# Sixteen high products, then sixteen low ones: the order inside a block of weights

## The chip, the core and the metric

The kernel runs on one core of one Trainium2 chip. The metric is the device time of one execution in microseconds (us). A core has a matrix engine (TensorE, PE in the profile, with its weight loads listed apart as PEld), three engines for elementwise work (VectorE or DVE, ScalarE or ACT, GpSimd or POOL), and queues that issue transfers (SP for SyncE).

## The reference

Two layers of a decoder act on 256 tokens of 1024 features, in float32. A layer is

```
h = rmsnorm(x); proj = h @ w_in            # 1024 -> 8192 columns: conv b, c, u; q, k; v, g; ga, gb
y_conv = short_conv(b, c, u) @ w_conv_out
y_ret  = (silu(g) * norm(retention(q, k, v))) @ w_ret_out
x = x + (sigmoid(ga) * y_conv + sigmoid(gb) * y_ret) @ w_o
x = x + square(relu(rmsnorm(x) @ w_up)) @ w_down   # 1024 -> 4096 -> 1024
```

and a last rmsnorm follows. Nearly all the work is the products with the weights: some 40 million multiplications per token and part, each weight used once against all 256 tokens.

## The kernel before

Activations are kept with features on the 128 partitions and tokens along the free axis. For accuracy every operand of a large product is held as two parts, a high one (the value cast to the fp32r type, ACT, line 99) and a low one (what the cast left over, DVE, line 100). A product then takes three terms: high by high, high by low, and low by high. `Parts.at(k)` gives the 128 features of tile k as `[high 256 tokens | low 256 tokens]`, 512 columns side by side.

The weights come from memory in 152 blocks of 1 MB, each 1024 rows by 256 columns, as 16 weight tiles of 128 x 128. `load_block` issues the transfer and splits the block in two halves: for each half one ACT cast makes the high part and one DVE subtraction makes the low part. `next_block` does this two blocks ahead (AHEAD = 2); there are three raw buffers and three buffers for the parts.

`proj` takes one block (or four, in the last product of a layer) against an activation. For weight tile (k, j) it issues two matmuls: the high weights against all 512 columns, into the whole PSUM bank j, and the low weights against the 256 high columns, into the second half of bank j. A matmul is always preceded by the load of its weights, so a block is 32 loads and 32 matmuls. PE therefore sees 512, 256, 512, 256 and so on. 140 of the 152 blocks pass through `proj`. The others are eight blocks of v through `proj_tokens` (four at the head of each layer), where the roles of weights and activation are exchanged, and four at the end through `proj_one`, where all matmuls have 256 columns. `collect` (ACT copy, DVE add) brings a result out of PSUM; `ps_main` has three buffers of two banks.

Between blocks `run_waiting` puts small products: scores and values of the retention, sums of squares (`column_sums`, lines 219 and 220, two 512-column matmuls one after the other, or two of 256).

The order of the instructions on each engine is not the text's alone: a planner replays the program with its own costs when it is built, and takes, among what it thinks ready, what comes first in the text. Where it thought an activation late, the matmuls stand in another order than the text's (the first block behind a norm, for one); elsewhere the text's order holds.

Of the kernel before, what the change touches and what calls it, by code (L numbers as in the profile page):

```python
# [18 lines left out]
P = 128  # L19
# [12 lines left out]

# Columns of w_in in the order in which they are used, 256 at a time.
Q0, K0, V0, G0, GA0, GB0 = 3072, 3584, 4096, 5120, 6144, 7168
# [8 lines left out]
BLOCKS_PER_LAYER = 32 + 4 * 3 + 16 + 16  # L43
# Layout of the per-feature parameters of a layer.
G_MIX, G_MLP, G_RET, W_CONV, PER_LAYER = 0, 8, 16, 24, 48
# [3 lines left out]
def trunk_kernel(ctx, tc, px, pos, w, cst, mask, out):  # L49
# [31 lines left out]
    class Parts:  # L81
        """1024 features of an activation as two parts whose sum is exact, side by side."""

# [18 lines left out]
    def block_tiles():  # L102
        """A block as it comes, [P, 16, 128], and as two parts whose sum is exact."""
        raw = raw_p.tile([P, 2 * KT, P], F32, tag="raw", name="raw")
        parts = parts_p.tile([P, 2, 2 * KT, P], F32R, tag="parts", name="parts")
        return raw, parts
# [22 lines left out]

    # Small products wait here until the products that hide their inputs' latency are under way.  # L130
    waiting = []
# [15 lines left out]
    def proj(act, n_blocks=1):  # L147
        """256 features of act @ w, features on the partitions: [P, 2, 2, T].

        The products of the high parts are at [:, :, 0], those with a low part at [:, :, 1].  # L150
        """
        ps = ps_main.tile([P, 2, 2, T], F32, tag="mm", name="ps")
        for b in range(n_blocks):
            blk = next_block()
            for k in range(KT):
                a = act[b].at(k)
                for j in range(2):
                    first, end = b == 0 and k == 0, b == n_blocks - 1 and k == KT - 1
                    mm(ps[:, j], blk[:, 0, 2 * k + j, :], a, first, False)
                    mm(ps[:, j, 1], blk[:, 1, 2 * k + j, :], a[:, 0], False, end)  # L160
            run_waiting()
        return ps

    def proj_one(act, plus, n_blocks=2):
        """128 features of act @ w, from blocks of 2048 rows, and the two parts of plus: [P, T]."""
        ps = ps_main.tile([P, T], F32, tag="mm", name="ps1")
        n = 2 * KT
        for b in range(n_blocks):
            blk = next_block()
            for k in range(n):  # L170
                a = act[(b * n + k) // KT].at(k % KT)
                mm(ps, blk[:, 0, k, :], a[:, 0], b == 0 and k == 0, False)
                mm(ps, blk[:, 0, k, :], a[:, 1], False, False)
                mm(ps, blk[:, 1, k, :], a[:, 0], False, b == n_blocks - 1 and k == n - 1)
            if b == 0:
                for part in range(2):
                    mm(ps, ident, plus[:, part], False, False)
            run_waiting()
        return ps

    def proj_tokens(act):
        """256 features of act @ w, tokens on the partitions: [P, 2 (tokens), 2, 256]."""
        ps = ps_main.tile([P, 2, 2, T], F32, tag="mm", name="ps")
        blk = next_block()
        for k in range(KT):
            a = act.at(k)
            for j in range(2):
                c = slice(j * P, (j + 1) * P)
                mm(ps[:, j], a[:, 0, c], blk[:, :, 2 * k:2 * k + 2, :], k == 0, False)
                mm(ps[:, j, 1], a[:, 1, c], blk[:, 0, 2 * k:2 * k + 2, :], False, k == KT - 1)  # L190
        run_waiting()
        return ps

    def collect(ps, t=None):
        """The sum of the two halves of a product."""
        t = t2("sum", "sum", 4) if t is None else t
        nc.scalar.copy(t, ps[:, :, 1, :])  # L197
        nc.vector.tensor_tensor(out=t, in0=ps[:, :, 0, :], in1=t, op=ALU.add)  # L198
        return t

    def newton(y, a, m):
        """y nearer to m ** -0.5"""
        nc.vector.tensor_tensor(out=a, in0=y, in1=y, op=ALU.mult)
        nc.vector.scalar_tensor_tensor(out=a, in0=a, scalar=-0.5, in1=m, op0=ALU.mult, op1=ALU.mult)
        nc.vector.scalar_tensor_tensor(out=y, in0=a, scalar=1.5, in1=y, op0=ALU.add, op1=ALU.mult)

    def rsqrt(y, v, scale, alloc):
        """y = (v * scale + EPS) ** -0.5: a start from the bits, and three Newton steps."""
        m, a = alloc("rs_m"), alloc("rs_a")
        nc.vector.tensor_scalar(out=m, in0=v, scalar1=scale, scalar2=EPS, op0=ALU.mult, op1=ALU.add)  # L210
        nc.vector.tensor_scalar(
            out=y.bitcast(I32), in0=m.bitcast(I32), scalar1=-0.5, scalar2=float(0x5F3759DF), op0=ALU.mult, op1=ALU.add
        )
        for _ in range(3):
            newton(y, a, m)

    def column_sums(o, hi, lo):
        """The sums over the partitions of hi + lo, on every partition of o."""
        nc.tensor.matmul(o, lhsT=ones, rhs=hi, start=True, stop=False)
        nc.tensor.matmul(o, lhsT=ones, rhs=lo, start=False, stop=True)  # L220

    class Norm:
        """RMSNorm whose per-token factor is applied behind the products."""

# [35 lines left out]
        def total(self):  # L260
            """The sum of the squares of each token, on every partition."""
            st = ps_misc.tile([P, T], F32, tag="misc", name=f"{self.name}_st")
# [9 lines left out]

# [1 line left out]
    nc.vector.memset(idle, 0.0)  # L274
    nc.vector.memset(eps, EPS)
    # Any function of the table that the first activations need.
    nc.scalar.activation(eps2, eps, AF.Square)
# [18 lines left out]
    ready.update((i, b[1]) for i, b in enumerate(begun))  # L296
    # The tensor engine's clock rises only under load.
    warm = ps_misc.tile([P, 2 * T], F32, tag="misc", name="warm")
# [10 lines left out]
    def rotation_tables():  # L309
# [21 lines left out]
        nc.gpsimd.tensor_tensor(out=sin_t, in0=u, in1=n_, op=ALU.mult)  # L331
        # The minus sign of the first half of the rows, and the two of the double angle.
        scale(sin_t, sin_t, cst_sb[:, 1:2])
# [3 lines left out]
    for layer in range(DEPTH):  # L337
# [5 lines left out]
        def factors(norm=norm):  # L343
            """Per token: the norm's factor and its square, and the rotation with one or both."""
            rsqrt(rr, norm.total(), 1.0 / D, lambda n: t2(n, "rs", 2)[:, 0, :])
# [6 lines left out]
        if layer == 0:  # L352
# [7 lines left out]
            later(5, nc.sync.dma_start, mask_sb, mask)  # L360
        # The first four blocks do not need them.
        later(4 if layer == 0 else 2, factors)

        qk = stile("qk")
        # What is used against 256 tokens is kept in two parts: [P, 2 (parts), head, ...].
        q_parts, v0_parts = (s8.tile([P, 2, HEADS, T], F32R, tag="s8", name=n) for n in ("q_parts", "v0_parts"))
# [97 lines left out]
        def head_sums(i):  # L464
            """Two heads: the mean of the squares of each token, and its root by table."""
            st = ps_misc.tile([P, 2, T], F32, tag="misc", name="var_ps")
# [7 lines left out]
        def head_out(i):  # L474
            """Two heads: their norm, its gain, and the gate."""
            rs = rm[:, 0, 2 * i:2 * i + 2, :]
# [118 lines left out]

# [1 line left out]
    gf = par_sb[:, DEPTH * PER_LAYER:DEPTH * PER_LAYER + KT]  # L597
# [21 lines left out]
    later(2, sums_of, norm.sum[:, 0, :], True, False)  # L619
    # Brings in the table of the square root ahead of its use.  # L620
    nc.scalar.activation(eps2, norm.sum[:, 0, 0:1], AF.Sqrt)
    for k in (KT - 2, KT - 1):
# [8 lines left out]
        else:  # L631
            sums_of(sq, False, True)
    # A square root by table is the start, one Newton step makes it exact to float32.
    m, r, a = (small.tile([P, 2], F32, tag=n, name=n) for n in ("fin_m", "fin_r", "fin_a"))
# [3 lines left out]
    for c in (slice(0, 1), slice(1, 2)):  # L638
        nc.vector.scalar_tensor_tensor(
            out=a[:, c], in0=r[:, c], scalar=m[:, c], in1=r[:, c], op0=ALU.mult, op1=ALU.mult  # L640
        )
    # -2 times the result; the matrix that spreads it is -1/2 times the identity.
    nc.vector.scalar_tensor_tensor(out=r, in0=a, scalar=3.0, in1=r, op0=ALU.subtract, op1=ALU.mult)
# [14 lines left out]

# [1 line left out]
def _feature_tiles(a):  # L660
    """[..., 1024] -> [128, ..., 8]: feature 128 k + p at [p, ..., k]."""
    a = a.reshape(a.shape[:-1] + (KT, P))
# [3 lines left out]
def _blocks(w, starts, width=256):  # L666
    """Blocks of [8 x 128 rows, 256 columns], each as [128, 8 * 256]."""
    out = []
# [61 lines left out]
```

## Time and profile before

| | |
|---|---|
| median of 3 runs | 896.24 us (895.91 to 896.86) |
| the profiled execution | its span of 896.8 us, first to last instruction, is all the time that the profile gives for it |
| PE busy | 880.4 us, 98% |
| DVE, ACT, POOL busy | 704.1, 503.0, 272.2 us |
| matmuls | 5092 |
| mean granted TensorE clock | 0.988 of full speed |

Matmuls overlap, so the busy time of PE only says that it hardly waits. What one costs is read from the distance between the starts of neighbours, or from a long piece of the chain that ended last: its microseconds by its count of matmuls.

### The profile page before, as it was taken

Reading aid. Unit: us, or ns where it says so; the run is one execution under the profiler, and the core shown is the slowest. Engines: PE = TensorE matmul, PEld = TensorE weight load, DVE = VectorE, ACT = ScalarE, POOL = GpSimd, SP = SyncE. Lnnn points to the kernel's source line nnn. Section 1 sums busy time; section 2 is a strip of 40 time slices with the busy share of each in tenths; the row PEclk is TensorE's granted clock in tenths of the full one; section 3 lists DMA queues with packets and bytes.
Section 4 is the critical chain, followed back from the end, with each engine's and each line's share of the span. In section 5 each row is a group of like instructions: output and inputs, shape, how many; then the busy total and the mean of one; then the engine's idle time right before and its main releaser. Section 6 shows DMA issues by size and latency. Waiting matters only on the chain.

```text
span 896.8 us, 12679 instructions
## 1 busy us (share of the span) xinstructions
PE 880.4 (98%) x5092; PEld 769.0 (86%) x5092; DVE 704.1 (79%) x790; ACT 503.0 (56%) x704; POOL 272.2 (30%) x174
## 2 busy tenths in 40 slices
PE   6999999999999999999999999999999999999996
PEld 4887888888888888888888888888888888888896
DVE  6999999997767976555579999999967888664451
ACT  4645565565455877544444466656644687764440
POOL 4895443261003332100026643415300323220010
PEclk7999999999999999999999999999999999999998
DMA  8544653546444655555545465445655546555521
GB/s 274 192 176 149 227 188 141 178 170 220 185 146 183 235 194 187 200 190 194 190 161 188 141 212 199 153 141 189 235 188 188 188 155 221 190 191 190 191 84 48
DMA packets 24250, 163.00 MB, mean 182 GB/s; under 512 B 2816, under 2 KB 3200, under 8 KB 4992
## 3 DMA queue, kind: packets, MB, share of 16 engines
q1 hardware_dynamic: 23904, 161.68, 50.8%
q8 instruction: 40, 0.66, 0.3%
q10 hardware_dynamic: 288, 0.52, 0.2%
q14 instruction: 18, 0.15, 0.0%
HBM read 161.14 MB, written 1.05 MB: 181 GB/s over the span
## 4 chain that ended last, share of the span: by engine, by line
PE 91%; DVE 3%; POOL 3%; DMA 1%; ACT 1%; issue 1%; SPq 1%; DVEq 0%; POOLq 0%; ACTq 0%
PE ps L145 88%; DVE parts L100 1%; PE o_ps L145 1%; DMA raw<-w 1%; POOL ang L326 1%; PE sc_ps L145 1%; POOL sum L394 1%; DVE rot L380 0%; POOL red L314 0%; DVE rot L379 0%; POOL ang L314 0%; ACT parts L99 0%; POOL v L394 0%; DVE mix L235 0%; POOL qk L381 0%
## 5 line engine op out<-in xcount | busy, mean ns | idle before, releaser
L100 DVE TENSOR_TENSOR parts<-raw,parts 128x1024 fp32r<-128x1024 f32 (+2 forms) x312 | 418.1, 1372 | 67.6 <-ACT parts L99 67.4
L99 ACT CAST parts<-raw 128x1024 fp32r<-128x1024 f32 (+2 forms) x312 | 304.8, 1029 | 110.4 <-PE ps L145 78.4
L145 PE MATMUL ps<-mix,parts 128*128 128x512 f32 (+1 forms) x1792 | 320.4, 339 | 1.8 <-DVE parts L100 1.7
L145 PEld LDWEIGHTS ps<-mix,parts 128*128 128x128 f32 x1792 | 274.4, 188 | 42.5 <-DVE parts L100 2.7
L145 PE MATMUL ps<-up,parts 128*128 128x512 f32 (+1 forms) x1088 | 179.4, 326 | 0.0
L145 PE MATMUL ps<-mlp,parts 128*128 128x256 f32 (+1 forms) x1024 | 178.5, 336 | 0.0
L145 PEld LDWEIGHTS ps<-up,parts 128*128 128x128 f32 x1088 | 159.1, 188 | 19.6
L145 PEld LDWEIGHTS ps<-mlp,parts 128*128 128x128 f32 x1024 | 155.4, 188 | 22.4 <-issue 0.2
L197 ACT COPY sum<-ps 128x512 f32<-128x512 f32 x88 | 51.4, 584 | 124.4 <-PE ps L145 124.4
L198 DVE TENSOR_TENSOR sum<-ps,sum 128x512 f32<-128x512 f32 x88 | 60.1, 683 | 62.9 <-ACT sum L197 62.8
L571 POOL TENSOR_TENSOR u<-u,rr2m 128x512 f32<-128x512 f32 x32 | 47.8, 1493 | 123.6 <-ACT u L581 106.1
L145 PE MATMUL ps<-parts,mix 128*128 128x512 f32 (+1 forms) x256 | 51.4, 362 | 5.7 <-DVE parts L100 5.7
L247 POOL TENSOR_TENSOR mix_sum<-mix_sum,sq 128x512 f32<-128x512 f32 x8 | 12.8, 1602 | 145.2 <-ACT sq L245 145.1
L145 PEld LDWEIGHTS ps<-parts,mix 128*128 128x128 f32 x256 | 42.8, 206 | 14.1 <-DVE parts L100 8.1
L247 POOL TENSOR_TENSOR mlp_sum<-mlp_sum,sq 128x512 f32<-128x512 f32 x6 | 12.7, 2110 | 132.7 <-ACT sq L245 132.7
L145 PE MATMUL ps<-yc,parts 128*128 128x512 f32 (+1 forms) x256 | 45.1, 338 | 0.0
L145 PE MATMUL ps<-yr,parts 128*128 128x512 f32 (+1 forms) x256 | 45.1, 338 | 0.0
L145 PE MATMUL ps<-mg,parts 128*128 128x512 f32 (+1 forms) x256 | 45.1, 338 | 0.0
L145 PEld LDWEIGHTS ps<-yr,parts 128*128 128x128 f32 x256 | 39.2, 188 | 5.6
L145 PEld LDWEIGHTS ps<-mg,parts 128*128 128x128 f32 x256 | 39.2, 188 | 5.6
L145 PEld LDWEIGHTS ps<-yc,parts 128*128 128x128 f32 x256 | 39.2, 188 | 5.6
L522 POOL TENSOR_TENSOR sum<-sum,rr 128x512 f32<-128x512 f32 x8 | 17.8, 2222 | 40.4 <-DVE sum L198 40.4
(171 smaller groups left out, 676.9 us busy)
## 6 DMA issues: line engine op xcount, KB each, us to landing
raw<-w SPq DMA_DIRECT2D x150, 1024.0 KB, 4.8
raw<-w SPq DMA_DIRECT2D x4, 256.0 KB, 7.1
px_sb<-px SPq DMA_DIRECT2D x2, 256.0 KB, 4.5
raw<-w SPq DMA_DIRECT2D x1, 512.0 KB, 8.1
mask_sb<-mask SPq DMA_DIRECT2D x1, 512.0 KB, 7.7
out<-o SPq DMA_DIRECT2D x2, 256.0 KB, 2.3
out<-o ACTq DMA_DIRECT2D x2, 256.0 KB, 2.5
px_sb<-px SPq DMA_DIRECT2D x1, 384.0 KB, 7.0
```

What stands on the lines that cost most here:

```text
L99: nc.scalar.copy(hi, src)
L100: nc.vector.tensor_tensor(out=lo, in0=src, in1=hi.bitcast(F32), op=ALU.subtract)
L145: nc.tensor.matmul(o, lhsT=a, rhs=b, start=start, stop=stop, skip_group_check=True)
L197: nc.scalar.copy(t, ps[:, :, 1, :])
L198: nc.vector.tensor_tensor(out=t, in0=ps[:, :, 0, :], in1=t, op=ALU.add)
L247: nc.gpsimd.tensor_tensor(out=self.sum, in0=self.sum, in1=sq, op=ALU.add)
L326: nc.gpsimd.tensor_tensor(out=ang, in0=ang, in1=r, op=ALU.subtract)
L394: nc.gpsimd.tensor_scalar(out=o_, in0=t[:, c, :], scalar1=mu[:, c:c + 1], scalar2=None, op0=ALU.subtract)
L522: nc.gpsimd.tensor_tensor(out=z, in0=z, in1=both(rr2), op=ALU.mult)
L571: nc.gpsimd.tensor_tensor(out=u, in0=u, in1=both(rr2), op=ALU.mult)
```

## The change

In `proj` the two matmuls of a weight tile no longer stand side by side. All 16 high weight tiles of the block are used first, then all 16 low ones. The matmuls, their operands and sums, the loads and the splits are the same. (The diff's other edits take away comments; the line numbers stay.)

```
 for b in range(n_blocks):
     blk = next_block()
     for k in range(KT):
-        a = act[b].at(k)
         for j in range(2):
-            first, end = b == 0 and k == 0, b == n_blocks - 1 and k == KT - 1
-            mm(ps[:, j], blk[:, 0, 2 * k + j, :], a, first, False)
-            mm(ps[:, j, 1], blk[:, 1, 2 * k + j, :], a[:, 0], False, end)
+            mm(ps[:, j], blk[:, 0, 2 * k + j, :], act[b].at(k), b == 0 and k == 0, False)
+    for k in range(KT):
+        for j in range(2):
+            end = b == n_blocks - 1 and k == KT - 1
+            mm(ps[:, j, 1], blk[:, 1, 2 * k + j, :], act[b].at(k)[:, 0], False, end)
     run_waiting()
```

## Rows read from the trace of the kernel before

**Rows 1.** The page: busy time by engine, and the chain that ended last, by line.
```profile
PE 880.4 (98%) x5092; PEld 769.0 (86%) x5092; DVE 704.1 (79%) x790; ACT 503.0 (56%) x704; POOL 272.2 (30%) x174
...
PE ps L145 88%; DVE parts L100 1%; PE o_ps L145 1%; DMA raw<-w 1%; POOL ang L326 1%; PE sc_ps L145 1%; POOL sum L394 1%; DVE rot L380 0%; POOL red L314 0%; DVE rot L379 0%; POOL ang L314 0%; ACT parts L99 0%; POOL v L394 0%; DVE mix L235 0%; POOL qk L381 0%
```

**Rows 2.** Windows: stretch, length, PE, PEld, DVE, ACT, POOL busy (count), clock, DMA.
```profile
80.70:290.00 209.30, 209.28 (x1207) 182.63 (x1208) 183.70 (x210) 120.20 (x168) 61.10 (x32) 1.00 0.50 181
290.00:862.00 572.00, 572.00 (x3308) 501.00 (x3307) 438.04 (x473) 333.66 (x458) 149.24 (x89) 1.00 0.53 188
```

**Rows 3.** Chain that ended last, whole span: start us, us, what (count).
```profile
98.87 5.65 PE ps L145 x32
...
289.20 174.80 PE ps L145 x1008
...
464.23 62.19 PE ps L145 x352
```

**Rows 4.** The same chain, cut to 185 to 284 us.
```profile
184.80 99.29 PE ps L145 x562
```

**Rows 5.** The same chain, cut to 590 to 700 us.
```profile
589.92 110.24 PE ps L145 x636
```

**Rows 6.** PE's timeline near 300 us: start, us, instruction (form of the first).
```profile
300.02 0.51 PE L145 MATMUL ps<-mlp,parts 128*128 128x256 f32 x2
...
300.13 0.51 PE L145 MATMUL ps<-mlp,parts 128*128 128x512 f32 x2
...
300.36 0.51 PE L145 MATMUL ps<-mlp,parts 128*128 128x256 f32 x2
...
300.48 0.51 PE L145 MATMUL ps<-mlp,parts 128*128 128x512 f32 x2
```

**Rows 7.** PE's timeline where three 512-column matmuls follow each other, twice.
```profile
144.08 0.39 PE L219 MATMUL var_ps<-osq,ones 128*128 128x512 f32 x1
144.31 0.39 PE L220 MATMUL var_ps<-osq,ones 128*128 128x512 f32 x1
...
144.54 0.39 PE L145 MATMUL ps<-mix,parts 128*128 128x512 f32 x1
...
150.19 0.40 PE L219 MATMUL var_ps<-osq,ones 128*128 128x512 f32 x1
150.42 0.40 PE L220 MATMUL var_ps<-osq,ones 128*128 128x512 f32 x1
...
150.66 0.40 PE L145 MATMUL ps<-mix,parts 128*128 128x512 f32 x1
```

**Rows 8.** Chain near 863 us (`proj_one`), cut at 869.0 and at 869.5.
```profile
862.91 6.11 PE ps L145 x51
...
862.91 6.59 PE ps L145 x55
```

**Rows 9.** PE's timeline near 20 us, granted clock at half.
```profile
20.00 0.63 PE L145 MATMUL ps<-parts,mix 128*128 128x512 f32 x1
...
20.42 0.84 PE L145 MATMUL ps<-parts,mix 128*128 128x256 f32 x2
```

**Rows 10.** PEld's timeline at its waits between 69 and 82 us.
```profile
73.30 0.19 PEld L145 LDWEIGHTS ps<-mix,parts 128*128 128x128 f32 x1 [0.43 <-ACT parts L99]
74.37 0.76 PEld L145 LDWEIGHTS ps<-mix,parts 128*128 128x128 f32 x5 [0.88 <-DVE parts L100]
...
80.72 1.35 PEld L145 LDWEIGHTS ps<-mix,parts 128*128 128x128 f32 x8 [0.84 <-DVE parts L100]
...
70.34 0.76 PEld L145 LDWEIGHTS ps<-mix,parts 128*128 128x128 f32 x5 [0.93 <-DVE parts L100]
```

**Rows 11.** DVE's timeline, the low parts of two blocks there.
```profile
73.11 3.44 DVE L100 TENSOR_TENSOR parts<-raw,parts 128x1024 fp32r<-128x1024 f32 x2
...
78.94 3.95 DVE L100 TENSOR_TENSOR parts<-raw,parts 128x1024 fp32r<-128x1024 f32 x2
```

## Prediction, before the changed kernel ran

> **What bounds the kernel now.** I read the page first. PE is busy for 98% of the span, and one line, the matmuls of the products, makes up 88% of the chain that ended last [rows 1]. The reader should not stop at "PE bound": a busy PE may be a slow or a waiting PE. So the table by stretches comes next: from 80.7 us to 862 us PE is busy all the time at the full granted clock (1.00, the 2.4 GHz level), while DVE is at 88% and then 77%, and the transfers at about half [rows 2]. For those 781 us the time is a count of matmuls times what one costs, and nothing else ends last. Only the first 80 us and the last 30 have another bound.
>
> What one costs is therefore the question, and the chain answers it, because its long pieces give microseconds and a count. There are two prices. In the MLP of the first layer 1008 matmuls take 174.80 us, 5.549 us for 32 of them, one block [rows 3]; from 590 to 700 us it is 110.24 us for 636, 5.547 us [rows 5]. But a block between two small products takes 5.65 us, 352 matmuls behind 464 us take 62.19, that is 5.654 [rows 3], and 562 matmuls around 230 us take 99.29, again 5.653 [rows 4]. The same work in the same order costs 346.7 ns or 353.3 ns per pair, and stays at one price until a small product comes in between. What the order and the phase of the starts do to PE is thus visible without the change: 2%.
>
> How many blocks are dear: 17.6 in [rows 4], 11 in the last row of [rows 3], and the first row of it stands for 16 (eight in each layer, between the scores and the values). With the ends of those stretches I take 46 of the 140. The mean of a block in `proj` is then (46 x 5.652 + 94 x 5.548) / 140 = 5.582 us.
>
> Inside a pair the starts tell the split. A 256 at 300.02, a 512 at 300.13, a 256 at 300.36, a 512 at 300.48: about 0.115 us after a 256 and 0.23 us after a 512 [rows 6]. At half clock (1.2 GHz level) a 512 is followed after 0.42 us [rows 9]. Two of these less are 0.21, and a 512 takes 0.23 at full clock: some 7 to 9% are lost at full clock that are not lost at half. [...]
>
> **The change, part by part.** It removes and adds no instruction: 16 loads with 16 matmuls of 512 columns and 16 with 256, per block, as before. Nothing moves on SP, ACT, DVE or POOL. Transfers and splits are issued where they were, and the parts are released by the block's last matmul, as before. What changes is the neighbour of each matmul, and when the low weights are first wanted.
>
> *Low products in a run.* The end of the kernel already has them: `proj_one` issues nothing but 256-column matmuls, each with a new weight load. Cut at 869.0 us the piece holds 51 matmuls in 6.11 us, cut half a microsecond later 55 in 6.59: 0.48 us for four, 0.120 each [rows 8]. That is dearer than the 0.115 beside a 512. The first few behind a 512 may still be at the lower price, so I take 0.1195 as the mean of sixteen: 1.912 us.
>
> *High products in a run.* No long run of 512s at full clock exists. The nearest are the two-matmul sums of the retention's norm, followed by a block that begins with a 512: starts at 144.08, 144.31, 144.54, and 150.19, 150.42, 150.66, so 0.23, 0.23, 0.23 and 0.24, mean 0.2325 [rows 7]. Beside a 256 a 512 takes 0.231 at the cheap price (0.3467 less 0.1155). I take 0.2315, between the two: 3.704 us for sixteen. The bounds: from above 0.24, the dearest of the four. From below 0.2267: if a pair goes on costing its cheap 0.3467 in sum and the low ones rise to 0.120, this is what is left for the high one.
>
> So a block becomes 3.704 + 1.912 = 5.616 us against 5.582: +0.034, and over 140 blocks +4.8 us. With the bounds: 16 x 0.2267 + 1.92 = 5.547 gives -4.9 us, 16 x 0.24 + 1.912 = 5.752 gives +23.8 us.
>
> *The low weights are wanted later.* In the first layer PE waits three times for DVE's low part of a block, 0.93, 0.88 and 0.84 us, and once 0.43 us at a block's start [rows 10]. Behind them PE is never idle up to 862 us [rows 2]. With sixteen high products ahead, the first low one comes 3.7 us after the block's start instead of 0.23. DVE delivers the two halves of such a block over 3.44 or 3.95 us, and the first lands about 1 us after PE begins the block [rows 10, 11]; the second, some 1.7 to 2 us later, is wanted at 4.7 us. All three waits are covered. But the first one (70.34) ends in a block behind which PE waits at 73.30 for something else, so coming 0.93 earlier would only lengthen that 0.43. I take the other two, 0.88 + 0.84 = 1.7 us, with bounds of 0 (PE, now ahead, meets the next late thing, such as a result that DVE has not yet taken out of PSUM) and 3.1 (all four). The cover is the run of high products; without it the waits come back at the same size. What PE gains there it keeps, since it bounds everything after.
>
> *Everything else* costs nothing here. The high part of the second half of a block and of the last features of an activation is wanted earlier: after 8 x 0.2315 = 1.9 us instead of 2.8. ACT makes it, and ACT is busy 57% and 58% [rows 2]. Where an activation is only just ready (behind a norm, before the output product), the planner already mixes the order by what it thinks ready, and can do so again with the low products, which want the high part of the activation alone; PE has no wait there now, and a misjudged one would cost under 1 us in each of some eight places. The last low product ends the block as before, so `collect` starts when it did.
>
> The sum: +4.8 - 1.7 = +3.1 us on the profiled 896.8, 899.9 us. That execution lies 0.6 us above the median of 896.24, so 899.3 us for the median.
>
> A rule of the Trainium skill speaks against any effect on the rate: "TensorE: Matmul & The Clock Gate", section "Step-by-step: what each phase is for", says that the moving operand and the weight load have SBUF read ports of their own, and that loading the next weights takes nothing from the running matmul. Its section "Back-to-back issue gap" gives N / 2.4 + 2.5 ns, by which a pair would take an estimated 215.8 + 109.2 = 325 ns in either order, and the sum would be the -1.7 us of waits alone. Here a pair takes 347 or 353 ns in one and the same order, so the trace doesn't agree, and I give the rule only the chance of the first rival.
>
> **The rivals.**
>
> *Order does not matter.* Runs cost on average what the mix costs, 5.582 us a block, and only the waits go: 896.2 - 1.7 = 894.5 us (893.1 to 896.2 with the waits' bounds). For it: all four distances of [rows 7] are near those beside a 256. Against it: two prices for one order.
>
> *Runs settle at the cheap price (faster).* In a run every neighbour is the same, and each block starts out of the same phase, so no stretch stays at the dear price: -4.9 - 1.7 = -6.6, 889.6 us. The mechanism sits in the 46 dear blocks, which lose 0.104 us each; it decides once the high run falls below 0.2295 us each. For it: the low run at exactly 0.120 for dozens of matmuls is one steady price. Against it: that price is the dearer one, and no 512 behind a 512 was below 0.23.
>
> *High runs at the dear end.* 0.24 each: +23.8 - 1.7, 918 us. Only one of four distances says so.
>
> *The planner undoes it.* It orders by what it thinks ready, and might pair high and low again, or put the next block's high products first. In the steady stretches the order is the text's, so I give this little; the time would be about as before.
>
> **How the numbers follow.** Within 0.2%, or 1.8 us, a change cannot be told from none here: 894.4 to 898.0 us. The forecast's case, a high run between 0.2305 and 0.235, gives blocks of 5.600 to 5.672 us and 897.0 to 907.1 us: chance 0.42, of it 0.05 within 0.2%. Order does not matter: 0.23, of it 0.11 faster and 0.12 the same. Cheap runs: 0.24, faster. Dear runs: 0.06. The planner: 0.05, the same. Together faster 0.35, same 0.22, slower 0.43. The range of 888 to 908 us takes in the forecast's own range (897 to 907) and the two rivals below it, and leaves out the dear runs and what lies under a high run of 0.226.
>
> **What would show it.** In the profile after: three or more consecutive 512s in a block with their distance (0.2315 expected, under 0.2295 for the faster rival); the 256s at 0.12; chain pieces of 5.62 us for 32 matmuls, and no longer two prices; no wait of PE's loads for DVE's parts between 69 and 82 us; and the same end of the span, 30 us behind the last block of `proj`. I am wrong if PE waits again in the middle of blocks (low weights or an activation that is late), if DVE's or ACT's order changes enough to move the end of the first 80 us by more than 3 us, or if a run of sixteen has a price that no pair of neighbours here shows.

## The result, and the profile after

The changed kernel takes 902.3 us (902.19 to 902.67, four runs) against 896.55 for the kernel before on the same chip: ratio 1.0059, interval 1.0045 to 1.0072. It is slower by 5.8 us. The prediction said 899.3 us, 888 to 908, with slower as the likeliest sign. The number and the sign hold. The reason given for them doesn't, as the profile shows. Its execution spans 900.2 us; the execution with its span inside took 902.36 us.

The page, busy time and the chain that ended last by line, to be held against [rows 1]. (I wrote that the line numbers stay; behind `proj` they are one higher in the changed kernel, so line 235 of before is 236 here.)

```profile
PE 879.0 (98%) x5092; PEld 775.5 (86%) x5092; DVE 705.0 (78%) x790; ACT 503.1 (56%) x704; POOL 272.5 (30%) x174
...
PE ps L145 75%; DVE parts L100 7%; DVE px_sb L556 1%; DMA raw<-w 1%; DVE mlp L236 1%; DVE sum L199 1%; POOL ang L327 1%; PE o_ps L145 1%; POOL red L315 1%; POOL sum L395 0%; DVE rot L381 0%; ACT parts L99 0%; DVE rm L478 0%; DVE acc L421 0%; DVE rot L380 0%
```

PE is busy for 1.4 us less than before, in a longer span. A kernel whose matmuls had become dearer would show more busy time, not less. And the products' line has 75% of the chain where it had 88%: there are places now in which PE waits, and the chain goes back through another engine from there.

The chain, cut to stretches in the MLP of the first layer (start us, us, what, count): ten blocks and one matmul; the sixteen high products of one block and one low one; five and ten of the high ones; fourteen of the low ones.

```profile
364.21 55.90 PE ps L145 x321
...
364.21 3.77 PE ps L145 x17
...
364.21 1.16 PE ps L145 x5
...
365.37 2.27 PE ps L145 x10
...
367.98 1.68 PE ps L145 x14
```

Less the one 512 of 0.23 us, ten blocks take 55.67 us, 5.567 each. In a run a 512 costs 0.232 us for the first five and then 0.227; a 256 costs 0.120. From the sixth on that is the faster rival's price for the high products (0.2267), which no pair of neighbours before had shown [rows 7]; the mean of the sixteen is 0.229. It holds where the alternating order was dear as well as where it was cheap: a block between two small products takes 5.58 us (before 5.65 [rows 3]).

```profile
526.77 5.58 PE ps L145 x32
```

So the work itself did not become dearer: 140 x (5.567 - 5.582) = -2.1 us against the first profile of before, an estimate that a second profile will make smaller. The loss is elsewhere. PE's load queue, from 38 to 870 us: what it waited for, us in total, times, longest. Before, this stretch had the waits of [rows 10].

```profile
PEld ps L145 <- DVE mlp L236: 5.1, 2, 2.5
PEld ps L145 <- ACT parts L99: 1.9, 1, 1.9
PEld ps L145 <- issue: 1.7, 2, 1.5
```

The waits for DVE's low parts of the weights are gone, as foreseen. In their place stands one in each layer on `mlp`, the normed activation that the MLP's first product reads. The timeline of PE, then of PEld, there (first layer, second layer):

```profile
272.39 3.82 PE L145 MATMUL ps<-mlp,parts 128*128 128x512 f32 x16
278.32 5.06 PE L145 MATMUL ps<-mlp,parts 128*128 128x512 f32 x21 [2.12 <-DVE mlp L236]
```

```profile
278.32 4.87 PEld L145 LDWEIGHTS ps<-mlp,parts 128*128 128x128 f32 x22 [2.54 <-DVE mlp L236]
...
712.54 6.47 PEld L145 LDWEIGHTS ps<-mlp,parts 128*128 128x128 f32 x22 [2.55 <-DVE mlp L236]
```

PE issues sixteen high products in 3.82 us, has nothing more that it may do, and stands until DVE has made the low part of more features. Before, it went through the same place with 41 matmuls in 7.46 us and no wait:

```profile
274.74 7.46 PE L145 MATMUL ps<-mlp,parts 128*128 128x512 f32 x41
```

DVE was no earlier then. Its timeline, before (the last four rows as one, and the first of them alone):

```profile
274.01 1.92 DVE L235 SCALAR_TENSOR_TENSOR mlp<-px_sb,mlp 128x256 fp32r<-128x256 f32 x2
...
279.92 2.10 DVE L235 SCALAR_TENSOR_TENSOR mlp<-px_sb,mlp 128x256 fp32r<-128x256 f32 x4
...
279.92 0.92 DVE L235 SCALAR_TENSOR_TENSOR mlp<-px_sb,mlp 128x256 fp32r<-128x256 f32 x1
```

and after:

```profile
272.69 1.31 DVE L236 SCALAR_TENSOR_TENSOR mlp<-px_sb,mlp 128x256 fp32r<-128x256 f32 x2
...
276.79 1.48 DVE L236 SCALAR_TENSOR_TENSOR mlp<-px_sb,mlp 128x256 fp32r<-128x256 f32 x1
...
279.45 0.89 DVE L236 SCALAR_TENSOR_TENSOR mlp<-px_sb,mlp 128x256 fp32r<-128x256 f32 x2 [0.18 <-ACT mlp L235]
```

A row with x1 is one of the eight feature tiles, and the first two are made earlier. Behind the first product that reads the activation (274.74 before, 272.39 after) the fourth tile's low part is there after 1.2 and 1.6 us, the fifth's after 6.1 and 5.9 us, the last one's after 7.3 and 8.0 us. What changed is how much PE can do until the fifth is there. Sixteen high products are 3.7 us of work, and 5.9 less 3.7 is the wait; the same sixteen with their low ones would be 16 x 0.347 = 5.6 us (both by the prices above). Sixteen fits four feature tiles, with two weight tiles each, in two blocks.

In the second layer the granted clock fell behind the wait in this execution. Windows: stretch, length, busy by engine, clock, DMA.

```profile
706.00:712.00 6.00, 4.42 (x23) 3.43 (x21) 6.00 (x8) 3.33 (x5) 3.21 (x2) 1.00 0.77 322
712.00:718.00 6.00, 5.46 (x17) 4.33 (x18) 2.79 (x6) 1.83 (x4) 2.21 (x3) 0.72 0.53 178
```

Over 6 us the mean is 0.72, which is part of the time at the half level (1.2 GHz): 6 x 0.28 = 1.7 us of full clock lost. The row of PE agrees: the 21 matmuls behind the wait take 6.66 us, where the same 21 in the first layer took 5.06. There, behind a wait of the same length, the clock stayed at 1.00.

```profile
712.54 6.66 PE L145 MATMUL ps<-mlp,parts 128*128 128x512 f32 x21 [2.12 <-DVE mlp L236]
```

### The profile page after: what moved, and what is told of

The parts are those of the page before. It is cut to its first block, busy times and chain, and to the rows that moved or that the text cites. A ratio compares the mean times of both kernels' runs of the same rounds, so it can differ in the third digit from the quotient of the medians.

```text
span 900.2 us, 12681 instructions
## 1 busy us (share of the span) xinstructions
PE 879.0 (98%) x5092; PEld 775.5 (86%) x5092; DVE 705.0 (78%) x790; ACT 503.1 (56%) x704; POOL 272.5 (30%) x174
## 4 chain that ended last, share of the span: by engine, by line
PE 76%; DVE 15%; POOL 4%; issue 3%; ACT 1%; DMA 1%; SPq 1%; DVEq 0%; POOLq 0%; ACTq 0%
PE ps L145 75%; DVE parts L100 7%; DVE px_sb L556 1%; DMA raw<-w 1%; DVE mlp L236 1%; DVE sum L199 1%; POOL ang L327 1%; PE o_ps L145 1%; POOL red L315 1%; POOL sum L395 0%; DVE rot L381 0%; ACT parts L99 0%; DVE rm L478 0%; DVE acc L421 0%; DVE rot L380 0%
## 5 line engine op out<-in xcount | busy, mean ns | idle before, releaser
L145 PE MATMUL ps<-mix,parts 128*128 128x256 f32 (+1 forms) x1792 | 317.5, 338 | 3.2 <-ACT parts L99 1.8
L145 PEld LDWEIGHTS ps<-mix,parts 128*128 128x128 f32 x1792 | 277.4, 190 | 40.6 <-ACT parts L99 1.9
L145 PE MATMUL ps<-mlp,parts 128*128 128x256 f32 (+1 forms) x1024 | 180.9, 339 | 4.2 <-DVE mlp L236 4.2
L145 PEld LDWEIGHTS ps<-mlp,parts 128*128 128x128 f32 x1024 | 158.6, 191 | 26.1 <-DVE mlp L236 5.1
L145 PE MATMUL ps<-up,parts 128*128 128x256 f32 (+1 forms) x1088 | 179.9, 327 | 0.0
L145 PEld LDWEIGHTS ps<-up,parts 128*128 128x128 f32 x1088 | 161.2, 190 | 18.1
L145 PE MATMUL ps<-mg,parts 128*128 128x256 f32 (+1 forms) x256 | 44.8, 336 | 0.0
```

The costliest lines, as they stand in the source:

```text
L145: nc.tensor.matmul(o, lhsT=a, rhs=b, start=start, stop=stop, skip_group_check=True)
```

## The experiments

Two theories went into them. *Waits:* the new order makes blocks slightly cheaper, and the kernel loses where low products of features that are ready stand behind high products of features that are late, behind the MLP's norm. *Rate:* runs cost more, as predicted. All kernels take `proj` with a length of run; KT is the change, 1 the order before (behind this text their line numbers are higher again):

```
-def proj(act, n_blocks=1):
+def proj(act, n_blocks=1, group=GROUP):      # GROUP = KT: the change; 1: before
...
+    for k0 in range(0, KT, group):           # group feature tiles: their high products, then their low ones
```

**Alternating only behind the norm.**

```
-collect(proj([norm.act]))
+collect(proj([norm.act], group=1 if p < 3 else KT))
```

> The new order everywhere, but the first three blocks of the MLP's first product alternate as before, in both layers. Waits theory (the time is lost where PE waits for the low part of the last features behind the norm, about 2.5 us in each layer and half-clock behind it in the second): no wait of PE over 1 us there, 895.5 to 898 us. Rate theory (runs of high products cost more, as I predicted): 6 of 140 blocks change, 901 to 902.5 us.

Measured: 896.56 us, ratio to before 1.0005 (0.9996 to 1.0015). With 6 of 140 blocks put back the whole loss is gone. PE's timeline has the same place without a wait, 80 matmuls in one piece:

```profile
271.38 14.71 PE L146 MATMUL ps<-mlp,parts 128*128 128x512 f32 x80
```

The other 134 blocks have the new order, so rate as the cause falls here. The interval also excludes a gain of 2.1 us by the cheaper blocks: none is to be seen against the kernel before as it ran beside this one.

**The reverse: the new order only there.**

```
-GROUP = KT
+GROUP = 1
-collect(proj([norm.act]))
+collect(proj([norm.act], group=KT if p < 3 else 1))
```

> The reverse: alternating everywhere as before, and the new order only in the first three blocks of the MLP's first product. Waits theory: PE waits there as in the changed kernel, 900.5 to 903 us. Rate theory: about 896.7 us, as before within 0.5 us.

Measured: 905.14 us, 1.0096 (1.0081 to 1.0111). Six blocks in the new order cost 8.7 us, more than all 140, and 2 us more than the upper end of the waits theory. The wait is there (1.39 us on PE's row, and the same in the second layer). It is the smaller part. The larger is the price of the blocks behind it: the MLP, cheap before [rows 3], is dear now in both layers, 155.12 us for 878, 5.654 a block, and 130.14 for 737. For some 55 blocks at 0.105 us that is an estimated 5.8 us. So this run shows that the six blocks bring the wait back, and not its size.

```profile
279.08 6.14 PE L146 MATMUL ps<-mlp,parts 128*128 128x512 f32 x26 [1.39 <-DVE px_sb L562]
```

```profile
294.92 155.12 PE ps L146 x878
```

```profile
729.98 130.14 PE ps L146 x737
```

**Runs of eight everywhere** (`GROUP = KT // 2`).

> Runs of eight: the high products of half a block, then its low ones, in every block. Waits theory: 8 high and 8 low products of the first half cover the last features instead of high ones alone, so the wait behind the norm falls to about half; a block costs 5.59 us (the first five 512s of a run are dearer), 898 to 901 us. Rate theory: about half of the change's loss, 899 to 900 us, with no change in the wait.

Measured: 900.38 us, 1.0046 (1.0031 to 1.0061), inside the range of the waits theory and 0.4 us above that of the rate theory, so the time alone hardly parts them. The wait does: on the norm's low parts it is 0.8 us in the first layer, against 2.5 in the changed kernel. PE has 32 products to go on with there, sixteen high and sixteen low ones, instead of sixteen. The waits are not the whole of this run's loss: a block costs 5.584 us (155.14 for 889), 0.017 more than in runs of sixteen, which is some 2.4 us over 140. (A row of the waits, of PE's timeline and of the chain.)

```profile
PEld ps L146 <- DVE mlp L242: 0.8, 1, 0.8
...
273.05 5.94 PE L146 MATMUL ps<-mlp,parts 128*128 128x512 f32 x32
...
294.97 155.14 PE ps L146 x889
```

**Alternating in the first layer's input product.**

```
-ps = proj(act)
+ps = proj(act, group=1 if layer == 0 else KT)
```

> Alternating in all blocks of the first layer's input product, the new order elsewhere. If the three waits for DVE's low parts in the first 82 us were really gained, as predicted, this loses 1.7 us against the change: 904 us. If what is gained there is given back at 176 us, where PE then waits for DVE to take a result out of PSUM: 902.3 us within 0.7.

Measured: 903.01 us, 1.0075 (1.0058 to 1.0092), between the two answers, with an interval that reaches over the changed kernel's. PE's waits up to 255 us are in this kernel

```profile
PE ps L146 <- DVE parts L101: 1.0, 2, 0.6
```

and in the changed one

```profile
PE ps L145 <- ACT parts L99: 1.8, 1, 1.8
PE ps L145 <- DVE ta L199: 1.3, 1, 1.3
```

The waits for DVE's parts that the change takes away come back as one for ACT's and one, at 177.7 us, for DVE to take the result `ta` out of PSUM. By the profiles the predicted 1.7 us are given back before 178 us. By the times alone 1.7 us more can't be excluded, since the intervals overlap.

**The kernel before, a second profile.**

> The kernel before once more, for a second profile (the same program). If the two prices of a block are set by the program, the same stretches are dear: 5.65 us a block from 185 to 284 us and from 464 to 526 us, 5.55 us from 290 to 455 us. If they are set by chance in each execution, other stretches are. Time 894 to 898.5 us.

Measured: 895.62 us in one run. Neither answer was right alone. The second layer's stretch is dear again to the digit (62.19 us for 352 [rows 3]); the stretch around 230 us, dear in [rows 4], is cheap now, 5.556 us a block:

```profile
184.89 99.14 PE ps L146 x571
```

```profile
461.38 62.19 PE ps L146 x352
```

```profile
91.97 5.55 PE ps L146 x32
```

So the alternating order falls to one of two prices by the program and by the execution, and the 46 dear blocks that I counted from one profile are not a fixed number. Counted over all pieces of the chain from 92 us on, they are some 52 in the first profile and some 31 here (four blocks between the scores of the first layer are cheap now too, 5.55 us), which makes this execution 21 x 0.104 = 2.2 us faster. With 31 dear ones a block costs 5.571 us, and the new order, at 5.567, gains 0.6 us in 140.

**Runs of four behind the norm** (`group=2 if p < 3 else KT`).

> The new order everywhere, but in the first three blocks of the MLP's first product in runs of four (four high products, four low ones of the same two feature tiles). If PE waits there because low products of features that are ready stand behind high products of features that are late, no wait over 0.5 us is left: 896 to 897.5 us, as with alternating blocks there. If it takes the strict alternation, for instance because a low product has to follow its high one at once, the wait stays: 901 to 902.5 us.

Measured: 897.23 us, 0.9996 (0.9987 to 1.0006), and one wait of 0.4 us left in the first layer. Strict alternation isn't needed. It is enough that the low products of two ready feature tiles don't stand behind the high ones of late tiles.

**The new order with nothing late.** The first three blocks of the MLP read the activation of the product before; the output changes with it.

```
-collect(proj([norm.act]))
+collect(proj([mg if p < 3 else norm.act]))
```

> The new order everywhere, and the first three blocks of the MLP's first product read the activation of the product before instead of the normed one (part of the computation is changed), so nothing there is late, with the same order. Waits theory: 895.5 to 897.5 us, the whole loss is gone though all 140 blocks keep the new order. If the order of those blocks costs something in itself: 901 to 902.5 us.

Measured: 895.74 us, 0.9981 (0.9972 to 0.9990). The order is the change's in all 140 blocks, the lateness is gone, and so is the loss.

**The same edit in the kernel before.**

> The kernel before (alternating everywhere), with the first three blocks of the MLP's first product reading the activation of the product before, as in the run of the new order with that edit (part of the computation is changed). If alternating blocks hide all of the lateness there, nothing is gained: as the kernel before within 0.5 us. If PE loses time there before the change too, it is 1 us or more faster.

Measured: 897.17 us, 0.9985 (0.9970 to 1.0000): the interval reaches from a gain of 2.7 us to none. That alternating blocks hide the lateness is therefore shown by the profile before, in which PE does not wait there [rows 2], and not by this time. Its runs spread from 892.49 to 898.84 us. The profiled one, at 892.49, had the second layer's stretch at the cheap price, 5.546 us a block, where both profiles of the kernel before had 62.19 us for 352 matmuls:

```profile
460.18 61.01 PE ps L146 x352
```

**Low products first behind the norm.** In the first three blocks of the MLP the two loops change places.

```
+for k in range(KT):
+    for j in range(2):
+        mm(ps[:, j, 1], blk[:, 1, 2 * k + j, :], act.at(k)[:, 0], k == 0, False)
+for k in range(KT):
+    for j in range(2):
+        mm(ps[:, j], blk[:, 0, 2 * k + j, :], act.at(k), False, k == KT - 1)
```

> The new order everywhere, but in the first three blocks of the MLP's first product the sixteen low products stand first and the sixteen high ones behind them. If the wait is what is left when the ready products of the leading run are used up, the leading run is now of 256-column products and gives PE half the work, 0.12 us each instead of 0.23: the wait grows by 1.5 to 3 us in each layer, 905 to 908 us. If the wait came from the low part of the activation, which low products don't read, it shrinks: 897 to 900 us.

Measured: 905.29 us, 1.0091 (1.0078 to 1.0104), slower than the change by some 2.9 us (by the two ratios), where 3 to 6 were expected of the waits theory, though low products read nothing that DVE makes of the activation. PE has 24 short products, some 2.9 us, instead of 16 long ones to go on with and waits twice. The second wait ends just behind DVE's row on `px_sb` (278.42 us), which takes the last result of the product before out of PSUM; that it makes the buffer for a third block free is my reading. (Rows of PE, and then that one of DVE.)

```profile
271.92 2.08 PE L146 MATMUL ps<-mlp,parts 128*128 128x256 f32 x16
274.62 1.21 PE L146 MATMUL ps<-mlp,parts 128*128 128x256 f32 x8 [0.62 <-ACT mlp L253]
278.56 12.56 PE L146 MATMUL ps<-mlp,parts 128*128 128x256 f32 x54 [2.73 <-DVE px_sb L574]
...
277.74 0.68 DVE L574 SCALAR_TENSOR_TENSOR px_sb<-ps,px_sb 128x512 f32<-128x512 f32 x1
```

**A version that keeps the gain:** alternating in the whole MLP, runs in the rest (input products, convolution and retention outputs, output product).

> The new order only where the alternating one was at its dear price (input products, convolution and retention outputs, output product), alternating in the whole MLP, up and down. Waits theory with prices set by the program: no wait behind the norm, 5.567 us a block in the first part and 5.547 us in the MLP, 893.5 to 895.5 us, faster than both kernels. If the MLP falls to the dear price behind runs of low products, 60 blocks at 5.65 us: 899 to 900.5 us.

Measured: 895.66 us, 0.9982 (0.9973 to 0.9991). It is faster than the kernel before by 0.2%, and than the change by some 0.8%. It lies 0.2 us above the expected range in time, and the MLP stays cheap. The new order with nothing late had 0.9981 beside the same runs of the kernel before, so I expect no more than this from the order. The kernel before itself has a median of 897.81 us here and had 896.41 beside the first runs; that its dear blocks make this difference is likely and not shown.

## Why the prediction was right in number and wrong in reason

The number is luck: two errors of some 7 us each, one in the rate and one in the waits, cancel.

*The rate: the term was mis-sized, with the wrong sign.* I had 16 x 0.2315 + 1.912 = 5.616 us a block and +4.8 us. The low products came as said, 0.120. The high ones cost 0.232 for five and then 0.227, 3.66 us for sixteen, so a block costs 5.567 and the term is -2.1 us. The step that failed is taking a run's price from pairs [rows 7]: these show what the first matmuls of a run cost, and those are the dear ones. The lower bound, 0.2267, worked out from a constant sum of a pair, was the price from the sixth on. This is the faster rival's rate, to which I gave 0.24; in the stretches looked at no dear one stays. The -2.1 us hang on the 46 dear blocks: by the first profile's own count of some 52 they would be -2.8, by the second profile's 31 they are -0.6. The sign of my +4.8 is wrong with each of them.

*The waits at the start: right in their place, not kept.* All three waits for DVE's parts went, and PE was ahead for a while. The bound of 0 that I named, a result that DVE has not yet taken out of PSUM, is what the profile shows at 177.7 us.

*"Everything else costs nothing": this step failed.* I wrote that behind a norm the planner could mix in low products, "which want the high part of the activation alone", and that a misjudged place would cost under 1 us. The profile has 2.5 us in each layer on the load queue (2.1 on PE's row, where ends are modelled), and 1.7 more by the clock in the second. The order that PE got shows why. In the 12 us from 272.4 the products on `mlp` are 43 of 512 columns and none of 256, although the inputs of low ones were there:

```profile
L145 PE MATMUL ps<-mlp,parts 128*128 128x512 f32 x43 | 10.2, 393 | 2.1 <-DVE mlp L236 2.1
```

That fits the text's order inside each block: no low product stands ahead of the block's last high one. Before, low products stood between high ones of the same block. I argue that the planner could not move them: all products of a bank add to the same PSUM, and the text now puts every high one first. That a low product may go early when the text lets it is shown by the runs of four (no loss) and by the runs of eight (0.8 us). That the wait grows when less ready work leads fits the low products first, with 2.9 us of it instead of 3.7 and waits of 0.62 and 2.73 us instead of 2.12; there the last wait ends with another event, so it is no clean measure of the size.

*The sum.* -2.1 + 5.1 + 1.7 = +4.7 us, with nothing left of the start's waits. The two profiled spans differ by 3.4 and the medians by 5.8. Against the second profile of the kernel before it is -0.6 + 5.1 + 1.7 = +6.2 us, and there the spans differ by 6.8 (900.2 and 893.4). The profiles differ from one execution to the next by the dear stretches (2.2 us between two of the kernel before) and by the clock of the first 22.6 us (0.70 before, 1.00 after), so a sum over one pair of them is not closer than about 2 us. The whole of the loss is settled by runs: put the order back in six blocks, or take the lateness away, and nothing of it is left. How often the clock falls behind the wait is open.

*The rivals.* That order doesn't matter came nearer for the rate than my own term did: 5.567 us a block against 5.582, or 5.571 by the second profile. Its 894.5 us failed by the waits behind the norm. The price that I took there from the Trainium skill, "TensorE: Matmul & The Clock Gate", section "Back-to-back issue gap", is not borne out: an estimate by its N / 2.4 + 2.5 ns, which the page gives for a matmul by itself, was 325 ns a pair in both orders, and a pair takes 347 or 353 ns in the old order and 348 in the new one (5.567 / 16). Whether weight loads take anything from a running matmul, no run here shows, since each matmul has one. High runs at 0.24 did not occur. The planner kept the text's order.

## What to carry to other kernels

A reordering inside the stream of the engine that bounds the kernel has two prices: what the steady state costs, and how much work that is ready stands ahead of work that is late. The first is read from pieces of the chain; for the second, walk to each place where an operand has only just been made, and count in us what the engine may still issue there. Here the first was worth between nothing and some 3 us of gain, by the execution of the kernel before, and the second about 7 us of loss. So long runs do no harm where nothing is late, and short ones belong behind a norm.

## What the runs showed that I had not expected

The alternating order has two prices for the same stretch. The stretch around 230 us took 5.653 us a block in one execution of the kernel before and 5.556 in another. The 352 matmuls behind the second layer's norm took 62.19 us in both, and 61.01 in the kernel with another activation behind the norm. One profile therefore tells which price a stretch had in that execution, and not which it has in the next. In long runs the price was the same in every block looked at: 0.232 us for the first five 512s, 0.227 for the rest, 0.120 for a 256.
